# A hybrid encoder layer on one Trainium2 core: the last down-projection product goes row by row in a fixed order, and the work behind it is rearranged

## The chip, the cores and the metric

The kernel runs on 1 core of one Trainium2 chip. The metric is the device time of one execution in microseconds (us), lower is better. Before the change it is 1217.25 us, the median of 3 runs (1216.84 to 1219.11). The names of the engines are those of the profile: PE multiplies matrices, DVE (VectorE) and ACT (ScalarE) work on whole tiles of 128 partitions, POOL (GpSimd) does small things here, SP only issues DMAs. [...]

## The reference

One layer of an encoder on a sequence of 1024 rows of 1024 numbers, in f32. What matters here is its end, the feed-forward part and the final normalisation:

```python
def rmsnorm(x, w):
    xf = x.astype(jnp.float32)
    y = xf * lax.rsqrt(jnp.mean(xf * xf, axis=-1, keepdims=True) + EPS)
    return (y * w.astype(jnp.float32)).astype(x.dtype)

def conv_ffn(h, w_up, conv_w, w_down):
    u = causal_dwconv(h @ w_up, conv_w)
    g, val = jnp.split(u, 2, axis=-1)
    return (jax.nn.silu(g) * val) @ w_down
...
        h = rmsnorm(x, norm_ffn_w[l]) * (1 + sc_f) + sh_f
        x = x + g_f * conv_ffn(h, w_up[l], ffn_conv_w[l], w_down[l])
    return rmsnorm(x, final_norm_w)
```

So at the end each row of x gets g_f times a row of the product with w_down added (the gate and the residual), then the mean of its squares is taken over all 1024 columns, and the row is scaled by one over the root of that mean and by the weights of the last norm.

## The kernel before

**Precision.** Products are in f32 made of three matmuls with rounded operands: each operand is split into a high part (rounded, a copy on ACT, line 85) and a low part (the rest, a subtraction on DVE, line 86). `mm3` multiplies high by high (line 76), high by low (77) and low by high (78), and adds all three in one PSUM bank.

**The product with w_down.** It runs as one level of a Strassen-Winograd scheme: seven products of half size instead of eight, called P1, Q5, Q6, Q7, Q4, P3 and P2 in their order. Each has 11 steps of 128 in the inner dimension (`KH` = 11), over four row tiles of 128 rows (`R4`) and 512 columns. A step is 12 matmuls of 128x512: four row tiles by three. Steps go in pairs: a pair m = 0 to 4 holds two steps, pair 5 (`NM` - 1) has one (`kn(m)`). For each pair both operands, a of w_down and b of the hidden rows, are loaded, added where the scheme wants it (line 1371), and split into a buffer of a ring of five (`ring`, `wsplit`, `split_pair`). So with two buffers for a pair, a pair's second buffer is free when PE is done with the pair two before it. The banks "d" and "e" of four each take turns: a product fills one set while the other is emptied.

**What is made of the products.** The output has eight row tiles, 0 to 7, in two halves of 512 columns. `q5` becomes the right half of tiles 4 to 7, `u3` the right half of tiles 0 to 3, `u2` the left half of tiles 4 to 7 and `p1` the left half of tiles 0 to 3. `p1` without its last addend, `q5` and `u3` are finished early and gated there (`gate`: times g_f, plus the residual x, which is loaded from `x1d`). `u2` waits for P3 (banks `Z`), and `p1` for P2 (banks `W`), the last product. Row tiles 4 to 7 are therefore finished beside P2, and tiles 0 to 3 only after it.

**The end of a row tile** is `final`: ACT squares both halves, with the sum as by-product (line 1431; the squares themselves go into one of three output buffers, `fins[st % 3]`, as junk), DVE adds the two sums and the epsilon (line 977), POOL raises that to the power -1/2 (line 978), DVE scales each half by it and by the norm's weights `fnr` (line 1434), and SP issues a DMA for each half (line 1436).

**Order.** The order on each engine is not that of the code: a scheduler arranges the instructions by a simulated timeline and by what each waits for. Helpers like `issue_after` and the wrapper `InOrder` pin an order: while `V.on`, `A.on`, `T.on` are set (DVE, ACT, PE), each instruction of that engine follows the one written before it; line numbers of such instructions are shown as L58. Before the change the end of the down-projection is left to the scheduler. Each engine works through its queue in order, so an instruction that waits holds up what stands behind it.

Of the kernel before, what the change touches and what calls it, by code (L numbers as in the profile page):

```python
# [12 lines left out]
AF = mybir.ActivationFunctionType  # L13
# [3 lines left out]
P = 128  # L17
# [47 lines left out]
def tile_block(ctx: ExitStack, tc: tile.TileContext, x, crep, pk, w_ada, w_first, w_ft, w_z,  # L65
# [1336 lines left out]

    def product(p, ps, ready=(), tail=False, between=None):
        last = []
        for m in RM:
            ab = ready[m] if m < len(ready) else split_pair(p, m)
            if between:
                between(m)
            for k in range(2 * m, 2 * m + kn(m)):
                if tail and m >= NM - 2:  # L1410
                    last.append((ab, k))
                else:
                    step(ps, ab, k, R4)
        return last

# [10 lines left out]

    def final(st, lo, hi):
        t = fins[st % 3]
        m = [stat(), stat()]
        for dh, src in enumerate((lo, hi)):  # L1430
            A.activation(t[:, halves[dh]], src, AF.Square, scale=1.0 / 32.0, accum_out=m[dh])
        r = rstd2(m)
        for dh, src in enumerate((lo, hi)):
            V.scalar_tensor_tensor(t[:, halves[dh]], src, r, fnr[:, halves[dh]], op0=ALU.mult,
                                   op1=ALU.mult)
            nc.sync.dma_start(out[st * P:(st + 1) * P, halves[dh]], t[:, halves[dh]])

# [54 lines left out]
    Z = banks("e")  # L1492
    product("P3", Z)
    W = banks("d")
    last = product("P2", W, tail=True)
    for st in R4:
        V.tensor_tensor(u2[st], u2[st], Z[st], ALU.add)
    for st in R4:
        gate(u2[st], 4 + st, 0)
        final(4 + st, u2[st], q5[st])  # L1500
    for st in R4:
        for ab, k in last:
            step(W, ab, k, (st,))
        e = xt_()
        V.tensor_tensor(e, W[st], gf[:, halves[0]], ALU.mult)
        V.tensor_tensor(p1[st], p1[st], e, ALU.add)
        final(st, p1[st], u3[st])
    es_s.close()
# [53 lines left out]
```

## Time and profile before

| what | value |
|---|---|
| median of 3 runs | 1217.25 us |
| the profiled execution, its own time | 1217.67 us |
| its span, from the first to the last instruction | 1215.9 us |
| mean granted TensorE clock | 0.991 |
| product P2 on PE: first matmul starts, last one starts | 1171.85, 1201.54 us |
| last scaling on DVE starts | 1212.05 us |

The profiled execution is one of its own, beside the three runs; 1217.67 - 1215.9 = 1.77 us lie around its span. All times in a trace count from the span's start. In a row of the timeline stand the start, the duration, the engine, the line, the operation, the tiles written and read, the shape and the count; in square brackets how long the engine stood idle before it and what ended that.

### The profile page before, as it was taken

To read this page: it belongs to the slowest core of one execution; us is meant where nothing else is said; L and a number is where in the kernel's file an instruction comes from. 1 tells how busy PE (TensorE), PEld (TensorE's weight loads), DVE (VectorE), ACT (ScalarE), POOL (GpSimd) and SP (SyncE) were. 2 spreads that over 40 slices of the span, in tenths; PEclk is the share of its full clock that TensorE was granted. 3 is DMA by queue.
4 is the path that set the end of the run, shared out by engine and by line. 5 is a ranking of instruction groups with operands and counts; after the bars stand their busy time and mean duration, and the time that the engine had idled before them with its cause. 6 is when DMAs were issued, how large, how long until landed. Compare 5 with 4: busy or idle time off the path is not lost.

```text
span 1215.9 us, 15656 instructions
## 1 busy us (share of the span) xinstructions
PE 1162.3 (96%) x5802; PEld 976.8 (80%) x5802; DVE 942.3 (77%) x1413; ACT 594.9 (49%) x1001; POOL 195.2 (16%) x174
## 2 busy tenths in 40 slices
PE   5999999999999989999899999999999999999995
PEld 4887888778889978888688888888888888888884
DVE  7756455598697788747899988988889779766976
ACT  4637465663333657676454543444434445433443
POOL 1109373782210134200000000000000000000002
PEclk9999999999999999999999999999999999999998
DMA  9632121323554301141223223322333278733533
GB/s 355 237 94 83 36 74 39 129 81 127 174 174 157 104 18 36 61 147 53 70 80 129 96 104 130 118 81 87 105 130 112 91 265 293 261 118 125 169 117 138
DMA packets 56683, 151.91 MB, mean 125 GB/s; under 512 B 5664, under 2 KB 5792, under 8 KB 55200
## 3 DMA queue, kind: packets, MB, share of 16 engines
q1 hardware_dynamic: 49552, 126.54, 31.3%
q10 hardware_dynamic: 7056, 24.38, 5.0%
q8 instruction: 45, 0.74, 0.3%
q14 instruction: 30, 0.25, 0.1%
HBM read 117.61 MB, written 29.10 MB: 121 GB/s over the span
## 4 chain that ended last, share of the span: by engine, by line
PE 67%; DVE 7%; ACT 2%; DMA 1%; issue 1%; POOL 0%; DVEq 0%; POOLq 0%; SPq 0%; ACTq 0%
PE dn L76 6%; PE dn L77 6%; PE dn L78 6%; PE wops L702 6%; PE uY L76 5%; PE uY L78 5%; PE uY L77 5%; PE uZ L78 3%; PE uZ L77 3%; PE uZ L76 3%; PE uX L78 3%; PE uX L77 3%; PE uX L76 3%; PE s L76 2%; PE s L77 2%; PE s L78 2%
## 5 line engine op out<-in xcount | busy, mean ns | idle before, releaser
L978 POOL TENSOR_TENSOR st<-st,mhalf 128x1 f32<-128x1 f32 x16 | 12.7, 799 | 691.7 <-DVE st L977 680.3
L76 PE MATMUL dn<-w 128*128 128x512 f32 x308 | 111.9, 389 | 0.0
L77 PE MATMUL dn<-w 128*128 128x512 f32 x308 | 111.9, 389 | 0.0
L78 PE MATMUL dn<-w 128*128 128x512 f32 x308 | 103.3, 389 | 0.0
L76 PE MATMUL uY<-tH,w 128*128 128x512 f32 x256 | 99.7, 390 | 1.8 <-ACT w L58 1.8
L410 POOL TENSOR_SCALAR p<-p,st 128x640 f32<-128x640 f32 (+4 forms) x64 | 98.5, 1554 | 13.6 <-DVE st L409 10.4
L78 PE MATMUL uY<-tH,w 128*128 128x512 f32 x256 | 99.6, 389 | 0.0
L77 PE MATMUL uY<-tL,w 128*128 128x512 f32 x256 | 99.6, 389 | 0.0
L85 ACT ACTIVATE w<-ya 128x1024 fp32r<-128x1024 f32 (+1 forms) x41 | 39.1, 955 | 86.1 <-PE uY L78 80.8
L702 PE MATMUL wops<-hH,yhl 128*128 128x512 f32 x224 | 74.9, 403 | 2.6 <-ACT yhl L85 1.4
L78 PEld LDWEIGHTS dn<-w 128*128 128x128 f32 x308 | 57.8, 188 | 12.1
L76 PEld LDWEIGHTS dn<-w 128*128 128x128 f32 x308 | 57.8, 188 | 12.0
L77 PEld LDWEIGHTS dn<-w 128*128 128x128 f32 x308 | 57.8, 188 | 11.9
L85 ACT ACTIVATE pt<-tp 128x512 fp32r<-128x512 f32 (+2 forms) x72 | 36.6, 523 | 48.6 <-PE tp L436 19.7
L404 DVE CUSTOM_DVE_ANT_0 p<-s,bias 128x640 f32<-128x640 f32 (+4 forms) x64 | 40.6, 650 | 25.4 <-PE tp L439 8.5
L86 DVE TENSOR_TENSOR pt<-tp,pt 128x512 fp32r<-128x512 f32 (+2 forms) x72 | 41.9, 595 | 22.3 <-ACT pt L85 13.4
L76 PEld LDWEIGHTS uY<-tH,w 128*128 128x128 f32 x256 | 48.0, 188 | 12.1 <-ACT w L58 2.2
L77 PEld LDWEIGHTS uY<-tL,w 128*128 128x128 f32 x256 | 48.1, 188 | 10.0
L78 PEld LDWEIGHTS uY<-tH,w 128*128 128x128 f32 x256 | 48.1, 188 | 9.9
L85 ACT ACTIVATE w<-xs 128x1024 fp32r<-128x1024 f32 (+1 forms) x41 | 38.9, 952 | 32.4 <-PE uY L78 32.4
L702 PEld LDWEIGHTS wops<-hH,yhl 128*128 128x128 f32 x224 | 42.4, 191 | 11.9 <-ACT yhl L85 1.7
L76 PE MATMUL s<-hH,wh 128*128 128x512 f32 x128 | 50.6, 395 | 0.9 <-DVE ct L515 0.9
(472 smaller groups left out, 3426.8 us busy)
## 6 DMA issues: line engine op xcount, KB each, us to landing
gz<-a ACTq DMA_DIRECT2D x10, 1024.0 KB, 5.3
wos<-in_w_ada_dram SPq DMA_DIRECT2D x18, 512.0 KB, 4.1
ya<-in_w_up_dram SPq DMA_DIRECT2D x11, 768.0 KB, 4.2
xs<-in_w_up_dram SPq DMA_DIRECT2D x11, 768.0 KB, 4.4
adat<-in_w_ada_dram SPq DMA_DIRECT2D x16, 512.0 KB, 6.4
raws<-in_w_ft_dram SPq DMA_DIRECT2D x16, 512.0 KB, 3.6
qk<-in_w_ada_dram SPq DMA_DIRECT2D x14, 512.0 KB, 4.4
gy<-a ACTq DMA_DIRECT2D x10, 512.0 KB, 2.6
```

The costliest lines, as they stand in the source:

```text
L76: T.matmul(ps, lh, rh, start=start, stop=False, skip_group_check=more)
L77: T.matmul(ps, lh, rl, start=False, stop=False, skip_group_check=more)
L78: T.matmul(ps, ll, rh, start=False, stop=stop, skip_group_check=more)
L85: i = A.activation(hi, src, AF.Copy) if ehi is A else ehi.tensor_copy(hi, src)
L86: return i, elo.tensor_tensor(lo, src, f32(hi), ALU.subtract)
L404: V.tensor_tensor_reduce(out=dst, in0=src, in1=bsl, scale=-1.0, scalar=3e38, op0=ALU.add, op1=ALU.min, accum_out=nm)
L410: G.tensor_scalar(pv_, pv_, rr, None, op0=ALU.mult)
L702: i = op(*a, **k)
L978: G.tensor_tensor(r, ms, mhalf[:, 0:1], ALU.pow)
```

## The change

The end of the kernel is rewritten from product P3 on. Nothing is computed otherwise; the order, the engine of some steps and a few buffers are other.

- **Fixed order.** For all of P2 and what stands beside and behind it, DVE, ACT and PE take the order of the code (`V.on = A.on = T.on = True`). Splits are made two pairs ahead.
- **P2 by row tile at its end.** Pairs 4 and 5 (three steps) are multiplied row tile by row tile: nine matmuls for tile 0, then nine for tile 1, and so on. The code before was written that way too, but the scheduler had interleaved the tiles.
- **One ring buffer for pair 5.** A pair of one step keeps both operands in one buffer, in all seven products.
- **Gates moved up.** The gate of `u2` is applied to what is there before P3 (times g_f, plus x, in `p3_rows`), and P3's result gets its own product with g_f (`add_gated`). This adds four multiplications of 128x512 on DVE. The right halves' squares are also taken early: those of tiles 4 to 7 in P3, those of tiles 0 to 3 in P2, where POOL also adds the epsilon.
- **Squares as junk into PSUM.** In P2 the squares go into the used banks `Z` and `W` instead of the output buffers.
- **The last row tiles.** `u3` is multiplied with the norm's weights beside P2. Behind P2 DVE multiplies and adds for a tile (`add_gated`), ACT squares it, POOL adds the two sums and takes the power, ACT scales the right half and issues its DMA, DVE scales the left half, and SP issues that DMA. The next tile's square stands ahead of the tile's scaling (`row_out(st - 1)`).

On DVE the end of the program stood as follows, from the first instruction that reads the last product (banks dn_9392 to dn_9395 are tiles 0 to 3, xs is a scratch row, cg is `p1`, dnH1 is `u3`):

```order
L1505 TENSOR_TENSOR xs_2856<-dn_9392,ya_781 128x512
L1505 TENSOR_TENSOR xs_2856<-dn_9393,ya_781 128x512
L1506 TENSOR_TENSOR cg_5464<-cg_5464,xs_2856 128x512 x2
L1505 TENSOR_TENSOR xs_2856<-dn_9394,ya_781 128x512
L1505 TENSOR_TENSOR xs_2856<-dn_9395,ya_781 128x512
L977 SCALAR_TENSOR_TENSOR st1_72<-st1_72 128x1
L1506 TENSOR_TENSOR cg_5464<-cg_5464,xs_2856 128x512
L977 SCALAR_TENSOR_TENSOR st1_72<-st1_72 128x1
L1506 TENSOR_TENSOR cg_5464<-cg_5464,xs_2856 128x512
L1434 SCALAR_TENSOR_TENSOR xs_2856<-cg_5464,st1_72,xs_2856 128x512
L1434 SCALAR_TENSOR_TENSOR xs_2856<-dnH1_8212,st1_72,xs_2856 128x512
```

With the change DVE's end is this, where the banks of tiles 0 to 3 are dn_9402 to dn_9405 (the first row is the low parts of pair 5, the second `u3` times the norm's weights):

```order
L58 TENSOR_TENSOR w_9552<-dna0_8320,w_9552 128x512 x2
L58 TENSOR_TENSOR dnH1_8212<-dnH1_8212,xs_2856 128x512 x4
L58 TENSOR_TENSOR xs_2856<-dn_9402,ya_781 128x512
L58 TENSOR_TENSOR cg_5464<-cg_5464,xs_2856 128x512
L58 TENSOR_TENSOR xs_2856<-dn_9403,ya_781 128x512
L58 TENSOR_TENSOR cg_5464<-cg_5464,xs_2856 128x512
L58 SCALAR_TENSOR_TENSOR xs_2856<-cg_5464,st1_72,xs_2856 128x512
L58 TENSOR_TENSOR xs_2856<-dn_9404,ya_781 128x512
L58 TENSOR_TENSOR cg_5464<-cg_5464,xs_2856 128x512
L58 SCALAR_TENSOR_TENSOR xs_2856<-cg_5464,st1_72,xs_2856 128x512
L58 TENSOR_TENSOR xs_2856<-dn_9405,ya_781 128x512
L58 TENSOR_TENSOR cg_5464<-cg_5464,xs_2856 128x512
```

Behind that stand two more scalings, of the left halves of tiles 2 and 3. All four multiplications came first before; now a tile's scaling stands between the additions of the next tile and the multiplication of the one after it, and the right halves' scalings and the sums (L977) are gone from DVE.

On ACT the last instructions stood like this before:

```order
L1431 ACTIVATE xs_2856,st1_72<-ya_781 128x512
L1431 ACTIVATE ya_781,st1_72<-dnH1_8212 128x512
L85 ACTIVATE w_9525<-dna0_8320 128x512
L1431 ACTIVATE xs_2856,st1_72<-dnH1_8212 128x512 x2
L1431 ACTIVATE xs_2856,st1_72<-cg_5464 128x512 x2
L1431 ACTIVATE ya_781,st1_72<-cg_5464 128x512
L1431 ACTIVATE xs_2856,st1_72<-cg_5464 128x512
L1431 ACTIVATE xs_2856,st1_72<-dnH1_8212 128x512
```

With the change ACT's last instructions are these; a row that writes dn is a square, one that writes xs or ya is a right half that is scaled:

```order
L58 ACTIVATE dn_9402,st1_72<-cg_5464 128x512
L58 ACTIVATE dn_9403,st1_72<-cg_5464 128x512
L58 ACTIVATE xs_2856<-dnH1_8212,st1_72 128x512
L1434 DMA out_0_dram<-xs_2856 128x512
L58 ACTIVATE dn_9404,st1_72<-cg_5464 128x512
L58 ACTIVATE xs_2856<-dnH1_8212,st1_72 128x512
L1434 DMA out_0_dram<-xs_2856 128x512
L58 ACTIVATE dn_9405,st1_72<-cg_5464 128x512
L58 ACTIVATE ya_781<-dnH1_8212,st1_72 128x512
L1434 DMA out_0_dram<-ya_781 128x512
L58 ACTIVATE xs_2856<-dnH1_8212,st1_72 128x512
L1434 DMA out_0_dram<-xs_2856 128x512
```

The squares of the right halves (dnH1) have left the end, four scalings and four DMA issues have come to ACT, and no square writes an output buffer there any more.

On PE the last matmuls of the program stood interleaved over the four banks before:

```order
L76 MATMUL dn_9392<-w_9522,w_9525 128x512
L77 MATMUL dn_9392<-w_9522,w_9525 128x512
L76 MATMUL dn_9393<-w_9522,w_9525 128x512
L77 MATMUL dn_9393<-w_9522,w_9525 128x512
L76 MATMUL dn_9394<-w_9522,w_9525 128x512
L77 MATMUL dn_9394<-w_9522,w_9525 128x512
L77 MATMUL dn_9395<-w_9516,w_9519 128x512
L78 MATMUL dn_9395<-w_9516,w_9519 128x512
L78 MATMUL dn_9392<-w_9522,w_9525 128x512
L78 MATMUL dn_9393<-w_9522,w_9525 128x512
L78 MATMUL dn_9394<-w_9522,w_9525 128x512
```

Now they go tile by tile, six matmuls of pair 4 and three of pair 5 for each:

```order
L58 MATMUL dn_9402<-w_9510,w_9513 128x512 x6
L58 MATMUL dn_9402<-w_9552 128x512 x3
L58 MATMUL dn_9403<-w_9510,w_9513 128x512 x6
L58 MATMUL dn_9403<-w_9552 128x512 x3
L58 MATMUL dn_9404<-w_9510,w_9513 128x512 x6
L58 MATMUL dn_9404<-w_9552 128x512 x3
L58 MATMUL dn_9405<-w_9510,w_9513 128x512 x6
L58 MATMUL dn_9405<-w_9552 128x512 x3
```

The number of matmuls is the same. The core of the diff:

```diff
     def split_pair(p, m):
-        ab = [wsplit(t, kn(m)) for t in operands(p, m)]
+        if kn(m) == 1:
+            w = ring()
+            ab = [w[:, :, j:j + 1, :] for j in range(2)]
+            for t, src in zip(ab, operands(p, m)):
+                last_split[:] = split(t[:, 0], t[:, 1], src, A, V)
+        else:
+            ab = [wsplit(t, kn(m)) for t in operands(p, m)]
...
+    def mean(src, junk):
+        m = stat()
+        A.activation(junk, src, AF.Square, scale=1.0 / 32.0, accum_out=m)
+        return m
+
+    def store(q, st, dh):
+        q.dma_start(out[st * P:(st + 1) * P, halves[dh]], fins[st % 3][:, halves[dh]])
+
+    def scale_row(st, src, r, dh):
+        V.scalar_tensor_tensor(fins[st % 3][:, halves[dh]], src, r, fnr[:, halves[dh]], op0=ALU.mult,
+                               op1=ALU.mult)
+        store(nc.sync, st, dh)
...
+    def p3_rows(m):
+        if m < 4:
+            gate(u2[m], 4 + m, 0)
+            mh[4 + m] = mean(q5[m], fins[m % 3][:, halves[1]])
+
+    product("P3", Z, between=p3_rows)
     W = banks("d")
-    last = product("P2", W, tail=True)
+    V.on = A.on = T.on = True
+    V.last = A.last = T.last = None
+
+    def add_gated(t, ps):
+        e = xt_()
+        V.tensor_tensor(e, ps, gf[:, halves[0]], ALU.mult)
+        V.tensor_tensor(t, t, e, ALU.add)
+
+    ml = {}
+    ab = [split_pair("P2", m) for m in range(2)]
+    for m in RM:
+        rs = {}
+        if m == 0:
+            for st in R4:
+                add_gated(u2[st], Z[st])
+                ml[4 + st] = mean(u2[st], Z[st])
+        elif m < 3:
+            rs = {st: rstd2([ml[4 + st], mh[4 + st]]) for st in (2 * m - 2, 2 * m - 1)}
+        if m + 2 < NM:
+            ab.append(split_pair("P2", m + 2))
+        for st in rs:
+            scale_row(4 + st, u2[st], rs[st], 0)
+            scale_row(4 + st, q5[st], rs[st], 1)
+            mh[st] = mean(u3[st], Z[st])
+            G.tensor_scalar(mh[st], mh[st], EPS, None, op0=ALU.add)
+        if m == 4:
+            for st in R4:
+                V.tensor_tensor(u3[st], u3[st], fnr[:, halves[1]], ALU.mult)
+        if m < NM - 2:
+            for k in range(2 * m, 2 * m + 2):
+                step(W, ab[m], k, R4)
+    rs = {}
+
+    def row_out(st):
+        A.activation(fins[st % 3][:, halves[1]], u3[st], AF.Copy, scale=rs[st])
+        store(nc.scalar, st, 1)
+        scale_row(st, p1[st], rs[st], 0)
+
     for st in R4:
-        V.tensor_tensor(u2[st], u2[st], Z[st], ALU.add)
-    for st in R4:
-        gate(u2[st], 4 + st, 0)
-        final(4 + st, u2[st], q5[st])
-    for st in R4:
-        for ab, k in last:
-            step(W, ab, k, (st,))
-        e = xt_()
-        V.tensor_tensor(e, W[st], gf[:, halves[0]], ALU.mult)
-        V.tensor_tensor(p1[st], p1[st], e, ALU.add)
-        final(st, p1[st], u3[st])
+        for k in range(2 * NM - 4, KH):
+            step(W, ab[k // 2], k, (st,))
+        add_gated(p1[st], W[st])
+        m, rs[st] = mean(p1[st], W[st]), stat()
+        G.tensor_tensor(m, m, mh[st], ALU.add)
+        G.tensor_tensor(rs[st], m, mhalf[:, 0:1], ALU.pow)
+        if st > 0:
+            row_out(st - 1)
+    row_out(3)
```

More of the change, by code (lines that the diff above doesn't have):

```diff
@@ L1401, in step, with product @@
             mm3(ps[st], b[:, 0, c], b[:, 1, c], a[:, 0, :], a[:, 1, :], k == 0, k == KH - 1)
-    def product(p, ps, ready=(), tail=False, between=None):
-        last = []
+    def product(p, ps, ready=(), between=None):
         for m in RM:
@@ L1409, in product @@
             for k in range(2 * m, 2 * m + kn(m)):
[L1410 to L1414, printed above, removed]
+                step(ps, ab, k, R4)
     def xt_():
@@ L1425, in gate @@
         V.tensor_tensor(t, t, x, ALU.add)
[L1427 to L1436, printed above, removed]
+    def mean(src, junk):
[8 more added lines that the diff above has]
+        store(nc.sync, st, dh)
     def rows(ts):
@@ L1492, in tile_block @@
     Z = banks("e")
[L1493 to L1507 removed]
+    mh = {}
```

## The prediction

> **What bounds the kernel now.** I read the page first, then the busy time of the last stages by windows, then the timeline of each engine behind the last product.
>
> ```profile
> span 1215.9 us, 15656 instructions
> PE 1162.3 (96%) x5802; PEld 976.8 (80%) x5802; DVE 942.3 (77%) x1413; ACT 594.9 (49%) x1001; POOL 195.2 (16%) x174
> 1010.00:1020.00 10.00, 10.00 (x46) 8.28 (x45) 10.00 (x10) 3.35 (x5) 0.00 (x0) 1.00 0.95 351
> 1190.00:1200.00 10.00, 10.00 (x46) 8.29 (x45) 5.01 (x8) 4.03 (x11) 2.47 (x2) 1.00 0.41 154
> 1200.00:1205.00 5.00, 1.93 (x9) 1.27 (x7) 4.17 (x8) 1.34 (x4) 0.34 (x1) 0.97 0.00 0
> 1205.00:1216.00 11.00, 0.00 (x0) 0.00 (x0) 6.48 (x13) 2.17 (x6) 2.36 (x4) 0.50 0.51 191
> ```
>
> In a window's row the second number is PE's busy time, the fourth DVE's, the fifth ACT's, the sixth POOL's; the last three are the granted clock, the DMA share and GB/s. PE is busy 96% of the span and wholly so until 1200, at full clock, so there is nothing to win ahead of the last matmul, only something to lose. Behind it PE has nothing left, and DVE works 6.48 of the last 11 us. That tail is what the change can shorten.
>
> ```profile
> 1171.85 0.39 PE L76 MATMUL dn<-w 128*128 128x512 f32 x1
> 1201.54 0.39 PE L78 MATMUL dn<-w 128*128 128x512 f32 x1
> 1200.83 1.29 DVE L1505 TENSOR_TENSOR xs<-dn,ya 128x512 f32<-128x512 f32 x2 [4.71 <-PE dn L78]
> 1202.04 1.28 DVE L1506 TENSOR_TENSOR cg<-cg,xs 128x512 f32<-128x512 f32 x2
> 1203.24 1.28 DVE L1505 TENSOR_TENSOR xs<-dn,ya 128x512 f32<-128x512 f32 x2
> ...
> 1205.78 0.74 DVE L1434 SCALAR_TENSOR_TENSOR xs<-cg,st,xs 128x512 f32<-128x512 f32 x1
> ...
> 1208.43 0.14 DVE L977 SCALAR_TENSOR_TENSOR st<-st 128x1 f32<-128x1 f32 x1
> 1209.24 0.75 DVE L1434 SCALAR_TENSOR_TENSOR ya<-cg,st,xs 128x512 f32<-128x512 f32 x1 [0.66 <-POOL st L978]
> ...
> 1211.38 0.75 DVE L1434 SCALAR_TENSOR_TENSOR xs<-cg,st,xs 128x512 f32<-128x512 f32 x1 [0.66 <-POOL st L978]
> 1212.05 0.75 DVE L1434 SCALAR_TENSOR_TENSOR xs<-dnH,st,xs 128x512 f32<-128x512 f32 x1
> 1208.66 0.63 ACT L1431 ACTIVATE xs<-cg 128x512 f32<-128x512 f32 x1 [2.72 <-DVE st L977]
> 1209.20 0.19 ACT L1431 ACTIVATION_READ_ACCUMULATOR xs<-cg 128x1 f32 x1
> ```
>
> The first two rows are the first and last of P2's 132 matmuls: (1201.54 - 1171.85) / 131 = 0.2266 us from one to the next. The last ends at 1201.54 + 0.39 = 1201.93. DVE sits idle for 4.71 us and begins only at 1200.83, because the four tiles come out of PE together. Then it has all four tiles to do at once: two instructions of 128x512 start 1.21 us ahead of the next two, so 0.60 each; a scaling takes 0.66 from start to start. It ends at 1212.05 + 0.75 = 1212.80, 10.87 behind PE, and 3.1 us later the span ends (DMA issue, landing, end of program). ACT's square of tile 3 waits 2.72 us. The row names L977, but that had long ended; tile 0's left scaling ends at 1205.78 + 0.74, its store lands 2.0 us on (next fence), at 1208.5, and the square starts at 1208.66: its junk goes into the buffer which that store reads. Together the tail is 1215.9 - 1201.93 = 13.97 us.
>
> ```profile
> out_dram<-xs SPq DMA_DIRECT2D x12, 256.0 KB, 2.0
> 1183.66 2.65 POOL L978 TENSOR_TENSOR st<-st,mhalf 128x1 f32<-128x1 f32 x2 [612.89 <-DVE st L977]
> 1189.86 2.07 POOL L978 TENSOR_TENSOR st<-st,mhalf 128x1 f32<-128x1 f32 x1 [3.54 <-DVE st L977]
> 1208.66 0.55 POOL L978 TENSOR_TENSOR st<-st,mhalf 128x1 f32<-128x1 f32 x1 [2.39 <-DVE st L977]
> 1189.70 1.22 DVE L86 TENSOR_TENSOR w<-dnL,w 128x1024 fp32r<-128x1024 f32 x1
> 1190.83 0.68 DVE L86 TENSOR_TENSOR w<-dna,w 128x512 fp32r<-128x512 f32 x1
> L116 POOL TENSOR_SCALAR st<-st x16: 213/255/634, 7.9 to 513.0; 128x1 f32<-128x1 f32 x16
> ```
>
> POOL's power takes 0.55 us alone. The one at 1189.86 took 2.07: it ends at 1191.93, 0.42 behind the second of two DVE subtractions of tiles in SBUF (1190.83 + 0.68 = 1191.51). So such DVE work holds POOL up, and I let a POOL operation that falls beside it end 0.42 after it.
>
> **The change part by part.** *PE.* The last product has the same 132 matmuls, so PE's last end stays at 1201.93 if nothing comes late. With the tiles one after the other, tile 3 ends there and tiles 2, 1 and 0 end 9, 18 and 27 matmuls earlier: 1199.9, 1197.9, 1195.8. Runs of 76, 77, 78 into one bank are in the old trace already at this pace, so I cost the new order of matmuls at nothing.
>
> *DVE up to tile 0.* Pair 4's second ring buffer is free when PE is done with pair 2; ACT's split of it starts then, also in the old trace:
>
> ```profile
> 1188.41 1.06 ACT L85 ACTIVATE w<-dnL 128x1024 fp32r<-128x1024 f32 x1 [2.82 <-issue]
> 1020.06 0.68 DVE L1148 TENSOR_TENSOR ya<-ya,xs 128x512 f32<-128x512 f32 x1
> 1020.66 0.68 DVE L1150 TENSOR_TENSOR xs<-xs,ya 128x512 f32<-128x512 f32 x1
> ```
>
> 72 matmuls from 1171.85 end at 1188.3, and the row has 1188.41. ACT ends at 1189.47, and DVE's low part runs 1189.5 to 1190.7. The power for tile 6 stands beside this DVE work, so it comes at 1190.7 + 0.42 = 1191.1. Then DVE does four scalings (tiles 6 and 7, 4 x 0.66: 1193.8), pair 5's two low parts (2 x 0.60: 1195.0) and four multiplications of `u3` (4 x 0.60: 1197.4). PE needs the second low part at 1195.4, one matmul ahead of tile 0's end: it comes 0.3 us early. The second and third row show that an instruction which reads what the one before it wrote starts 0.60 behind it, so a multiplication and its addition cost 1.2.
>
> *The tail.* DVE reaches tile 0 at 1197.4, 1.6 late: DVE, not PE, is the bound from here. Tile 0: multiply 1197.4, add 1198.0; tile 1: 1198.6 and 1199.2, done at 1199.9. ACT squares tile 0 from 1198.7 (0.54 + 0.19 by its two rows). POOL's addition for tile 0 is held up by tile 1's: 1199.9 + 0.42 = 1200.3, and the power 0.55 + 0.03 behind it: 1200.9. DVE scales tile 0 (to 1201.55), multiplies and adds tile 2 (to 1202.75), scales tile 1 (its power came at about 1202.0; to 1203.4), multiplies tile 3, and adds it from 1204.0 to 1204.7. Now the last chain: square 0.73 (1205.45), POOL's addition and power with their releases 1.15 (1206.6), ACT's and DVE's scalings side by side 0.75 (1207.4). With the same 3.1 us behind it the span ends at 1210.5, which is **5.4 us less**.
>
> What goes is thus 5.4 of the 10.87: four right-half scalings (2.6) and four sums (0.3) leave DVE's tail, two tiles are multiplied and added under PE, and the wait of 2.72 on the store is gone, since squares write PSUM. What comes is POOL's second operation on the chain (0.55) and DVE being 1.6 late.
>
> *Not shown by the trace.* POOL's addition of two single columns: between 0.25 (the median of L116, the scalar addition) and 0.55 (the power); I take 0.55, the same kind of instruction. It counts twice, so 0.6 less is possible. The power for tile 6 may slip in between two subtractions: 0.4 less. A square that writes PSUM: between 0.52 (ACT copies out of PSUM, four in 2.07 us, third row of the next fence) and the 0.73 of a square with its read into SBUF; I take 0.73. The Trainium skill (ScalarE: Activation LUTs, section "Step-by-step: what each stage is for") says PSUM is the faster destination for ACT; no run here shows it, and by that the sum would be shorter by no more than the bound just given.
>
> *Hidden.* The four added multiplications (2.4 us of DVE) and the gates of `u2` stand in P3 and P2, where DVE has room: 5.01 of 10 in the window from 1190, and PE covers it. In P2 the adds of `Z` stand ahead of pair 2's split: low part of pair 1 done and DVE free at 1172.7 (buffer free at 1169.3 as P3's pair 4 ends, two ACT copies, two subtractions), eight instructions to 1177.5, the last square 0.63, two ACT copies 1.9, low parts to 1181.7. PE needs that one at 1171.85 + 50 x 0.2266 = 1183.2. So 1.5 us are left there; without that cover each us costs one.
>
> *DMA issues on ACT.*
>
> ```profile
> 1020.74 1.04 ACT L85 ACTIVATE w<-dnt1h 128x1024 fp32r<-128x1024 f32 x1
> 1020.77 0.33 ACTq L1149 DMA_DIRECT2D gy<-ya  x1
> 1021.76 2.07 ACT L1464 ACTIVATE cg<-dn 128x512 f32<-128x512 f32 x4
> DMA to landing us min/median/max: 2.0/2.6/5.3
> ```
>
> An issue on ACT runs beside ACT's work, and the next instruction starts without a gap. Tile 1's store waits for its scaling and stands ahead of tile 3's square, but both are done by 1204.7. SP has four issues fewer, one of them the last but one, so by the 0.33 of an issue at most 0.3 is gained. The last row is of the loads and stores of x1d.
>
> **A rule of the skill.** The slow powers above fit the Trainium skill (SBUF — State Buffer, section "Who interferes with whom"): a DVE instruction with two inputs in SBUF and a GpSimd instruction that reads SBUF exclude each other, the first to start keeps the shared ports to its end. The trace agrees for POOL behind DVE (2.07 against 0.55). The rule also says that POOL can hold up DVE, which no row here shows; it is the first rival below.
>
> **The rivals.**
> 1. *POOL and DVE block each other in every tile.* If a tile's POOL pair never ends before the next tile's addition plus 0.42 + 0.58, each scaling comes 1.0 behind that addition. For tile 1 that is 1203.85 for 1202.75, so 1.1 later, and the last addition on POOL waits 0.25 more: gain 4.1. For it: the 2.07. Against: for tile 1 POOL has the gap from 1200.9 to 1202.15, in which DVE scales and reads PSUM. Time 1213.2.
> 2. *PE gets gaps.* The scheduler has reordered DVE in P1 too, and there it is busy 10.00 of 10.00 (the window from 1010). One DVE instruction of 1.2 us too late, three times, gives PE 3.6 us of gaps; two loads of x that land in 5.3 instead of 2.6, ahead of P2's splits, take 0.9 beyond the 1.5 of cover. Against: no wait of PE in the old trace, and one ring buffer less per product gives the splits more time. Gain 1.8: 1215.5.
> 3. *The change doesn't do what it says*: the output buffer again. Tile 3 uses tile 0's; its stores are issued at about 1201.6 and land by 1203.6, or 1206.9 at 5.3, which would cost 0.3. Time 1212.2.
> 4. *Slower: squares into PSUM are dear.* Nothing in this trace shows ACT writing PSUM. In P2 pair 2's split stands behind four of them on ACT: at x us each they end at 1174.0 + 4x, and the low part is there 3.4 later; PE stalls from x = 1.45. Each further us costs 4 there and 1 in the tail. The gain of 5.4 is gone at x = 2.4, and at x = 3 PE stalls 6.2 and the tail adds 2.3: 3.1 slower, 1220.4. Against: reading PSUM costs ACT no more than SBUF does (0.52).
>
> **How the numbers follow.** The sum is made against the profiled execution: 1217.67 - 5.4 = 1212.3. That execution is 0.42 above the median of the three runs, 1217.25, which is what the result will be set against, so 1211.9. The rivals' times are set down by the same median. The forecast has a chance of 0.72, rival 1 0.10, rival 2 0.10, rival 3 0.04, rival 4 0.04. The bounds of the unknown costs reach 1.0 to 1.3 below (1210.6); the three runs alone lie 0.4 below and 1.9 above their median. Upwards the range takes in rivals 1 and 3 and some of 2: 1210.6 to 1214.6. A measurement can tell about 0.2% (2.4 us) from no change; forecast and rivals 1 and 3 are beyond it: faster 0.86, within 0.2% most of rival 2: 0.09, slower 0.05.
>
> **What would show it.** Right: PE without gaps to its last matmul about 1202 into the span; DVE's first reading of P2 about 4 us ahead of that; the last DVE scaling 5.5 behind it (10.87 before); no ACT square waiting for an output DMA. Wrong: PE gaps at P2's pair 2 or 5 (late low parts), squares over 1 us, POOL operations of 2 us in the last tiles, or a last scaling that waits for something other than POOL.

## The result, and the profile after

| what | before | after |
|---|---|---|
| median of 6 runs each | 1217.45 us (1216.84 to 1221.3) | 1213.02 us (1211.37 to 1214.02) |
| ratio, 95% interval | 1 | 0.9958 [0.9945, 0.9971] |
| the profiled execution, its time and its span | 1217.67, 1215.9 us | 1214.02, 1212.3 us |
| PE's last matmul ends | 1201.93 | 1203.63 |
| tail: from there to the span's end | 13.97 | 8.67 |

The change makes the kernel faster: by 4.4 us by the medians, by 5.1 (3.5 to 6.7) by the ratio. The profiled execution after, at 1214.02, is the slowest of its six runs. The prediction was 1211.9 us in a range of 1210.6 to 1214.6, with a gain of 5.4 and a tail of 8.6. The tail is there almost to the digit; as the experiments show, two errors in it cancel.

The profiled execution after has these rows on the page and in the windows (columns as before the change: PE, PEld, DVE, ACT, POOL, clock, DMA share, GB/s):

```profile
span 1212.3 us, 15660 instructions
PE 1163.7 (96%) x5802; PEld 977.8 (81%) x5802; DVE 945.7 (78%) x1413; ACT 597.0 (49%) x1005; POOL 197.0 (16%) x182
1190.00:1200.00 10.00, 10.00 (x46) 8.29 (x45) 9.72 (x15) 3.33 (x7) 3.62 (x4) 1.00 0.41 153
1200.00:1205.00 5.00, 3.63 (x16) 2.66 (x15) 4.20 (x7) 3.00 (x8) 2.33 (x5) 1.00 0.27 103
1205.00:1213.00 8.00, 0.00 (x0) 0.00 (x0) 2.48 (x4) 2.54 (x5) 1.42 (x4) 0.60 0.53 198
```

The busy totals hardly moved (DVE 942.3 to 945.7): the work is the same, it stands elsewhere. In the window from 1190 DVE went from 5.01 to 9.72 of 10 us, under PE; in the last window it does 2.48 where it did 6.48. The timeline of PE, DVE, ACT and POOL at the end:

```profile
1191.68 11.95 PE L58 MATMUL dn<-w 128*128 128x512 f32 x52
...
1192.31 0.75 DVE L58 SCALAR_TENSOR_TENSOR xs<-cv,st,xs 128x512 f32<-128x512 f32 x1
...
1198.57 0.68 DVE L58 TENSOR_TENSOR xs<-dn,ya 128x512 f32<-128x512 f32 x1
1199.29 0.69 DVE L58 TENSOR_TENSOR cg<-cg,xs 128x512 f32<-128x512 f32 x1
...
1200.61 0.69 DVE L58 TENSOR_TENSOR cg<-cg,xs 128x512 f32<-128x512 f32 x1
1202.03 0.75 DVE L58 SCALAR_TENSOR_TENSOR xs<-cg,st,xs 128x512 f32<-128x512 f32 x1 [0.73 <-POOL st L1549]
...
1205.41 0.69 DVE L58 TENSOR_TENSOR cg<-cg,xs 128x512 f32<-128x512 f32 x1
...
1207.78 0.75 DVE L58 SCALAR_TENSOR_TENSOR xs<-cg,st,xs 128x512 f32<-128x512 f32 x1 [1.02 <-POOL st L1549]
...
1206.13 0.60 ACT L58 ACTIVATE dn<-cg 128x512 f32<-128x512 f32 x1 [0.65 <-DVE cg L58]
...
1207.50 0.34 ACTq L1434 DMA_DIRECT2D out_dram<-ya  x1
1207.94 0.72 ACT L58 ACTIVATE xs<-dnH,st 128x512 f32<-128x512 f32 x1 [0.47 <-POOL st L1549]
...
1200.88 0.47 POOL L1548 TENSOR_TENSOR st<-st 128x1 f32<-128x1 f32 x1 [7.10 <-ACT dn L58]
...
1202.14 0.69 POOL L1548 TENSOR_TENSOR st<-st 128x1 f32<-128x1 f32 x1
...
1206.93 0.19 POOL L1548 TENSOR_TENSOR st<-st 128x1 f32<-128x1 f32 x1 [1.17 <-ACT dn L58]
1207.20 0.55 POOL L1549 TENSOR_TENSOR st<-st,mhalf 128x1 f32<-128x1 f32 x1
```

PE runs without a gap to 1191.68 + 11.95 = 1203.63. DVE takes up tile 0 at 1198.57, 5.06 ahead of that (1.10 before: 1200.83 against 1201.93). The last chain is then short: the addition of tile 3 (1205.41), its square (1206.13), POOL's addition and power (1206.93, 1207.20), and the two scalings side by side, DVE's to 1208.53 and ACT's to 1208.66.

**Why the tail gained 5.3 and the span only 3.6.** PE's end came 1.70 later. That is not the change. The first matmul of line 76 into `uX`, in code that is the same in all these kernels, shows it. In the timeline of before:

```profile
611.53 0.39 PE L76 MATMUL uX<-b11h,w 128*128 128x512 f32 x1
```

In that of after:

```profile
613.18 0.39 PE L76 MATMUL uX<-b11h,w 128*128 128x512 f32 x1
```

After is 1.65 later already there, hundreds of us ahead of the changed code. In the experiments below the same matmul starts anywhere from 608.38 (first bytes early) to 615.41 (add from PSUM). The windows show how this arises. In before, from 430 us to that matmul:

```profile
430.00:611.00 181.00, 172.29 (x862) 143.59 (x861) 132.64 (x185) 113.97 (x243) 34.21 (x41) 0.98 0.19 65
```

In the execution that was there at 608.38:

```profile
430.00:608.40 178.40, 169.65 (x863) 141.59 (x862) 132.45 (x186) 113.72 (x243) 33.73 (x41) 1.00 0.19 65
```

The granted clock is 0.98 in the one and 1.00 in the other, and the same matmuls keep PE busy 172.29 and 169.65 us. The clock isn't lowered evenly. It is 1.00 nearly everywhere and drops to 0.50 for some 3.4 us at a time: in before the windows of 2 us from 398 to 404 have 0.79, 0.50 and 0.86. Ahead of the `uX` matmul before has three such drops (near 400, 445 and 585 us), after has four, and the execution that was there at 608.38 has one. The fourth of after stands where before has none. First before, then after:

```profile
236.50:241.50 5.00, 3.95 (x29) 3.19 (x29) 3.35 (x10) 3.67 (x10) 5.00 (x4) 1.00 0.92 372
236.50:241.50 5.00, 4.66 (x28) 4.39 (x25) 2.64 (x8) 2.97 (x9) 5.00 (x3) 0.66 1.01 406
```

With three drops more than the execution at 608.38, after reaches the `uX` matmul 613.18 - 608.38 = 4.80 later, 1.6 for each drop; with one more than before, 1.65 later. What sets a drop off is not shown. So a single execution of any of these kernels lies some us up or down with the clock that was granted in the middle of the program. One execution per kernel can't judge a us by its time, but it can by its tail, which starts anew at PE's end. The experiments are read by the tail. Spans are given to 0.1, and three kernels with the same chain behind PE (the changed one, squares in buffers, store on SP) have tails of 8.62 to 8.67, so 0.3 is clear and 0.1 is not.

### The profile page after: what moved, and what is told of

The parts are those of the page before. It is cut to its first block, busy times and chain, and to the rows that moved or that the text cites. A ratio compares the mean times of both kernels' runs of the same rounds, so it can differ in the third digit from the quotient of the medians.

```text
span 1212.3 us, 15660 instructions
## 1 busy us (share of the span) xinstructions
PE 1163.7 (96%) x5802; PEld 977.8 (81%) x5802; DVE 945.7 (78%) x1413; ACT 597.0 (49%) x1005; POOL 197.0 (16%) x182
## 4 chain that ended last, share of the span: by engine, by line
PE 67%; DVE 7%; ACT 2%; DMA 1%; issue 1%; POOL 0%; SPq 0%; ACTq 0%; DVEq 0%; POOLq 0%
PE wops L702 6%; PE dn L76 5%; PE dn L78 5%; PE dn L77 5%; PE uY L76 5%; PE uY L77 5%; PE uY L78 5%; PE uZ L77 3%; PE uZ L76 3%; PE uZ L78 3%; PE uX L77 3%; PE uX L78 3%; PE uX L76 3%; PE s L76 2%; PE s L77 2%; PE s L78 2%
## 5 line engine op out<-in xcount | busy, mean ns | idle before, releaser
L978 POOL TENSOR_TENSOR st<-st,mhalf 128x1 f32<-128x1 f32 x12 | 9.8, 822 | 672.9 <-DVE st L58 625.0
L77 PE MATMUL dn<-w 128*128 128x512 f32 x264 | 97.8, 389 | 0.0
L76 PE MATMUL dn<-w 128*128 128x512 f32 x264 | 97.2, 389 | 0.0
L78 PE MATMUL dn<-w 128*128 128x512 f32 x264 | 92.1, 389 | 0.0
L78 PEld LDWEIGHTS dn<-w 128*128 128x128 f32 x264 | 49.6, 188 | 10.4
L77 PEld LDWEIGHTS dn<-w 128*128 128x128 f32 x264 | 49.6, 188 | 10.3
L76 PEld LDWEIGHTS dn<-w 128*128 128x128 f32 x264 | 49.5, 188 | 10.2
```

The costliest lines, as they stand in the source:

```text
L76: T.matmul(ps, lh, rh, start=start, stop=False, skip_group_check=more)
L77: T.matmul(ps, lh, rl, start=False, stop=False, skip_group_check=more)
L78: T.matmul(ps, ll, rh, start=False, stop=stop, skip_group_check=more)
L978: G.tensor_tensor(r, ms, mhalf[:, 0:1], ALU.pow)
```

## The experiments

Each is the changed kernel with one edit, if nothing else is said. PE's end is the start of the last group of matmuls in the timeline plus its duration.

| kernel | PE's end | span | tail | time (median) |
|---|---|---|---|---|
| the changed kernel | 1203.63 | 1212.3 | 8.67 | 1213.02, 6 runs |
| tiles together | 1193.63 + 12.18 = 1205.81 | 1217.5 | 11.69 | 1215.56, 10 runs |
| scheduler's order | 1201.93 + 0.39 = 1202.32 | 1212.2 | 9.88 | 1213.94, one |
| no square ahead | 1193.71 + 8.55 = 1202.26 | 1216.2 | 13.94 | 1216.91, 10 runs |
| squares in buffers | 1193.62 + 10.36 = 1203.98 | 1212.6 | 8.62 | 1214.35, one |
| right halves on DVE | 1193.70 + 7.42 = 1201.12 | 1210.4 | 9.28 | 1212.09, one |
| two ring buffers | 1184.82 + 17.44 = 1202.26 | 1211.5 | 9.24 | 1213.18, one |
| u3 in P3 | 1184.84 + 18.29 = 1203.13 | 1210.8 | 7.67 | 1211.32, 6 runs |
| add from PSUM | 1184.80 + 21.02 = 1205.82 | 1214.2 | 8.38 | 1215.9, one |
| last right half on DVE | 1189.66 + 12.40 = 1202.06 | 1210.8 | 8.74 | 1212.5, one |
| store on SP | 1189.77 + 11.27 = 1201.04 | 1209.7 | 8.66 | 1211.42, one |
| first bytes early (on u3 in P3) | 1189.78 + 9.00 = 1198.78 | 1206.3 | 7.52 | 1210.34, 6 runs |

### What the gain hangs on: the tiles' order on PE

```diff
+    for k in range(2 * NM - 4, KH):
+        step(W, ab[k // 2], k, R4)
     for st in R4:
-        for k in range(2 * NM - 4, KH):
-            step(W, ab[k // 2], k, (st,))
         add_gated(p1[st], W[st])
```

> The changed kernel with the last three steps of P2 multiplied step by step over all four tiles, not tile by tile; all else as changed. The tail (end of the last matmul to the end of the span) was 13.97 us before and 8.67 changed. Theory A, the order of the tiles on PE is what lets DVE start early: tile 0 ends 9 x 0.2266 = 2.0 us ahead of PE's end where it was 6.1, so DVE's first multiplication moves from 5.06 ahead of PE's end to 2.0 ahead, and everything behind it with it: tail +3.0, 11.7 us, time about 1216. Rival B, the gain is the work taken off DVE (right halves and sums, 2.9 us): the order of tiles matters little, since DVE was 1.1 us late for tile 0 anyway; tail +0 to +1.

Measured: the tail is 3.02 longer, and against before the ratio is 0.9994 [0.998, 1.0008]: no difference left that the time can tell, though the tail is still 2.3 shorter than before. DVE's first row of the tail:

```profile
1203.80 0.69 DVE L58 TENSOR_TENSOR xs<-dn,ya 128x512 f32<-128x512 f32 x1 [2.98 <-PE dn L58]
```

DVE was ready at 1200.8 and waited 2.98 for PE, to begin 2.0 ahead of PE's end instead of 5.06. Theory A holds with its number.

The second kernel leaves the order of DVE, ACT and PE to the scheduler.

```diff
-    V.on = A.on = T.on = True
-    V.last = A.last = T.last = None
```

> The fixed order of DVE, ACT and PE is taken away at the end; all else of the change stays, and the scheduler decides. It then interleaves the tiles on PE and puts DVE's first four multiplications in pairs ahead of most scalings. Theory A (the fixed order carries part of the gain): DVE begins tile 0 about 1.1 us ahead of PE's end and has seven instructions of 0.60 to 0.66 up to the last addition's end, 4.4 behind PE; with square 0.8, POOL 0.8, scaling 0.75 and 3.7 for the store the tail is about 10.5 us, 1.8 more than 8.67. Rival B (the moved work alone carries the gain): tail 8.7 to 9.2.

Measured: tail 9.88, 1.21 longer. The fixed order carries part of the gain, less than theory A's 1.8. Its start was wrong: DVE began 2.9 ahead of PE's end, not 1.1, when tiles 0 and 1 were both done.

```profile
1199.41 1.29 DVE L1507 TENSOR_TENSOR xs<-dn,ya 128x512 f32<-128x512 f32 x2 [5.62 <-PE dn L78]
```

### The next tile's square ahead of the scaling

```diff
-        if st > 0:
-            row_out(st - 1)
-    row_out(3)
+        row_out(st)
```

> The changed kernel with each tile's scaling straight behind its own square and power, so that the next tile's multiplication stands behind it on DVE and its square behind it on ACT. Theory A, having the next tile's work in the gap of POOL's power is worth most of the gain: per tile DVE waits for square 0.73, POOL's addition and power with their releases 0.9, so 1.6 us of idle for each of tiles 0 to 2 where it had 0.73 once: about 3 x 1.6 - 0.7 = +4.1, tail 12.8, nearly the old time (1217). Rival B, work taken off DVE: DVE's work is the same as in the changed kernel, so tail +0 to +1 (1213 to 1214).

Measured: tail 13.94, 5.27 longer, ratio to before 0.9998 [0.9984, 1.0011]. The whole gain is gone. The rows of DVE's first and last scaling of the tail:

```profile
1200.39 0.75 DVE L58 SCALAR_TENSOR_TENSOR xs<-cg,st,xs 128x512 f32<-128x512 f32 x1 [1.77 <-POOL st L1549]
...
1211.68 0.75 DVE L58 SCALAR_TENSOR_TENSOR xs<-cg,st,xs 128x512 f32<-128x512 f32 x1 [1.68 <-POOL st L1549]
```

Between them stand two more of 1.68. DVE goes the round of square, sum and power once for each tile, (1211.68 - 1200.39) / 3 = 3.76 us, where the changed kernel pays it in full only at the end. Theory A was right in kind and 1.2 short in size.

### Where the squares go, and the ring buffer

```diff
-        m, rs[st] = mean(p1[st], W[st]), stat()
+        m, rs[st] = mean(p1[st], fins[st % 3][:, halves[0]]), stat()
```

> The changed kernel with the squares of the last four tiles written into the output buffers, as before the change, not into PSUM. By the prediction's sentence that the wait of 2.72 us is gone since squares write PSUM, it comes back: ACT's square of tile 3 waits for tile 0's left store, tail +1 to +2.7. Theory A': the order of tiles removed it. Tile 0's left half is scaled 4.1 us ahead of tile 3's square now, its store lands 2.0 to 2.7 us behind its issue, so it is done 0.6 us ahead of the square: tail +0.0 to +0.1.

Measured: tail 8.62, the same. The prediction put the loss of the 2.72 us wait on the store down to the squares in PSUM (the memory of the product banks, which PE writes and DVE and ACT read in these traces); that is refuted. Tile 3's square again writes the buffer of tile 0, but tile 0's left half is now scaled by 1203.15 (1202.40 + 0.75), ahead of the additions of tiles 2 and 3, and a store lands 2.0 to 2.7 us on in this run, so by 1205.9. ACT's row waits for the addition alone:

```profile
1206.51 0.63 ACT L58 ACTIVATE xs<-cg 128x512 f32<-128x512 f32 x1 [0.66 <-DVE cg L58]
```

It takes 0.63 into SBUF, against the 0.60 into PSUM shown above. The Trainium skill (ScalarE: Activation LUTs, section "Step-by-step: what each stage is for") calls PSUM the faster destination; the trace agrees, by 0.03 us, which the tail doesn't show.

The next kernel gives pair 5 two ring buffers again (`ab = [wsplit(t, kn(m)) for t in operands(p, m)]` in all cases).

> Pair 5 takes two ring buffers again, as before the change. Theory A (the single buffer is needed by the row-by-row end): the second buffer is free only when PE is done with pair 3, which is 36 matmuls of 0.2266 us or 8.2 us ahead of PE's end; ACT's copy (0.5) and DVE's low part (0.6) follow, so DVE's four multiplications of u3 start 0.5 us later than in the changed kernel, and tile 0 with them: tail 9.2 instead of 8.67, PE without gaps of over 0.3. Rival B (there is room): tail within 0.15 of 8.67. Rival C (PE itself waits for the late low part): a gap of 0.5 or more ahead of pair 5's first matmul for tile 0.

Measured: tail 9.24, 0.57 longer, as theory A has it: DVE's second low part of pair 5 waits for ACT, which waited for PE. PE has a gap of 0.49 too, which theory A excluded and rival C looked for at another place. It is at P2's pair 2:

```profile
1194.75 0.69 DVE L58 TENSOR_TENSOR w<-dna,w 128x512 fp32r<-128x512 f32 x1 [0.53 <-ACT w L58]
...
1171.35 11.49 PE L58 MATMUL dn<-w 128*128 128x512 f32 x50
1183.33 6.87 PE L58 MATMUL dn<-w 128*128 128x512 f32 x29 [0.49 <-DVE w L58]
```

After 50 matmuls of P2 the low part of pair 2 is missing. That is the place where the prediction saw 1.5 us of cover: with two buffers DVE is busy with the splits of pairs 0 and 1 until 1173.78, 2.4 behind P2's start, and only then begins to add P3's banks; with the change's single buffer it begins 0.8 behind P2's start, and PE doesn't wait. The gap moves PE's end by itself, so it adds to the 0.57 of the tail.

### Right halves on ACT, and what the end of the stores is worth

In the first kernel the right halves are scaled on DVE as before the change, and the four multiplications of `u3` are gone.

```diff
-        if m == 4:
-            for st in R4:
-                V.tensor_tensor(u3[st], u3[st], fnr[:, halves[1]], ALU.mult)
...
-        A.activation(fins[st % 3][:, halves[1]], u3[st], AF.Copy, scale=rs[st])
-        store(nc.scalar, st, 1)
         scale_row(st, p1[st], rs[st], 0)
+        scale_row(st, u3[st], rs[st], 1)
```

> The changed kernel with the right halves of tiles 0 to 3 scaled on DVE and stored by SP as before the change, and without the four early multiplications by the norm's weights, which that makes needless. Theory A: DVE gets 2.4 us less ahead of the tail and 2.6 more in it. Its first multiplication comes 1.0 earlier (then PE's tile 0 is the bound), each of three tiles adds 0.66 and the last one 0.66 behind the left half: tail +0.4 to +0.8, 9.1 to 9.5 us. Rival B, the 2.6 us of right halves taken off DVE are half the gain: tail +2.6, 11.3 us.

Measured: tail 9.28, 0.61 longer: theory A. The 0.61 is a balance. Without the four multiplications DVE begins tile 0 at 1195.04, 6.08 ahead of PE's end, as it does in the kernel with `u3`'s work beside P3 (below), which keeps the right halves on ACT and has a tail of 7.67. Against that one the right halves on DVE cost 9.28 - 7.67 = 1.61. The last two rows:

```profile
1205.84 0.75 DVE L58 SCALAR_TENSOR_TENSOR xs<-cg,st,xs 128x512 f32<-128x512 f32 x1 [0.71 <-POOL st L1545]
1206.51 0.75 DVE L58 SCALAR_TENSOR_TENSOR xs<-dnH,st,xs 128x512 f32<-128x512 f32 x1
```

The last scaling ends at 1207.26, 6.14 behind PE, where the changed kernel has 4.90 on DVE: 1.24 later, for 0.61 of tail. From the last scaling to the end of the span are 3.14 us here, as before the change (3.1), and 3.64 in the changed kernel (from ACT's scaling; 3.77 from DVE's). From the *first* scaling of tile 3 it is 1210.4 - 1206.59 = 3.81 here, 1212.3 - 1208.53 = 3.77 after, and before 1215.9 - (1211.38 + 0.75) = 3.77. The DMA view says why. For the changed kernel, its share of busy time from 1207.5 to 1213 in 40 slices of 0.1375 us, and the stores issued there with their size and landing time:

```profile
DMA  1899989899930299999999980000000000000000
out_dram<-ya ACTq DMA_DIRECT2D x1, 256.0 KB, 2.0
out_dram<-xs SPq DMA_DIRECT2D x1, 256.0 KB, 2.1
out_dram<-xs ACTq DMA_DIRECT2D x1, 256.0 KB, 2.6
```

For the kernel with the right halves on DVE, from 1206 to 1210.5 in slices of 0.1125 us:

```profile
DMA  9999893000002799999999999300000000000000
```

The last block of 9s is the two stores of tile 3. It lasts 10 slices in the first and 12 in the second, 1.4 us in both and without a hole: 0.52 MB at some 370 GB/s. Whether the second half is scaled beside the first or 0.66 behind it, the bytes of the two take one stretch of 1.4 us that begins with the first. To test that, tile 3's right half alone went to DVE, behind the left half:

```diff
+        if st < 3:
             A.activation(fins[st % 3][:, halves[1]], u3[st], AF.Copy, scale=rs[st])
             store(nc.scalar, st, 1)
         scale_row(st, p1[st], rs[st], 0)
+        if st == 3:
+            V.tensor_scalar(fins[0][:, halves[1]], u3[3], rs[3], None, op0=ALU.mult)
+            store(nc.sync, 3, 1)
```

> The changed kernel, with the right half of tile 3 alone scaled on DVE behind the left half (a plain product with the power, since u3 holds the weights), instead of beside it on ACT. Theory A (the bytes bound the end): the left half's store starts when it did, the right half's bytes queue behind it as they do now, and the tail stays at 8.67, within 0.15, with only 3.1 to 3.2 from the last scaling's end to the span's end instead of 3.6 to 3.8. Rival B (the end follows the last scaling): 0.5 to 0.66 later, tail 9.2 to 9.3.

```profile
1206.24 0.75 DVE L58 SCALAR_TENSOR_TENSOR xs<-cg,st,xs 128x512 f32<-128x512 f32 x1 [1.03 <-POOL st L1553]
1206.91 0.48 DVE L58 TENSOR_SCALAR xs<-dnH,st 128x512 f32<-128x512 f32 x1
```

Measured: tail 8.74, the same within 0.07, though the last scaling ends 1207.39 - 1202.06 = 5.33 behind PE, for 5.03 in the changed kernel (ACT's, 1208.66). Theory A holds, rival B falls, though by less than was written: this form of the scaling takes 0.48, not 0.66, so the last scaling came only 0.30 later, and B asks for 8.97 instead of 9.2 to 9.3. From the last scaling to the span's end are 3.4 for the same reason, not 3.1 to 3.2; from the first, 1210.8 - 1206.99 = 3.81. The Trainium skill says the same of the two queues (DMA: Bandwidth & Descriptors, section "Issuing engines are not separate DMA queues"): stores issued by two engines share the DMA engines, only issue time is saved.

The next kernel moves the store of tile 2's right half from ACT, where it stands ahead of tile 3's scaling, to SP.

```diff
-        store(nc.scalar, st, 1)
+        if st != 2:
+            store(nc.scalar, st, 1)
         scale_row(st, p1[st], rs[st], 0)
+        if st == 2:
+            store(nc.sync, st, 1)
```

> The changed kernel, with the store of tile 2's right half issued by SP (behind that of the left half) instead of by ACT ahead of tile 3's scaling there. Theory A (ACT's issue holds ACT's next instruction): tile 3's scaling on ACT starts within 0.05 of POOL's power instead of 0.16 behind it. By the bytes the tail changes by less than 0.1, since DVE's store starts the flow. Rival B (the issue runs beside ACT's work, and the 0.16 has another reason): the 0.16 stays. Rival C (ACT's scaling sets the end): tail 8.5.

```profile
1204.62 0.55 POOL L1552 TENSOR_TENSOR st<-st,mhalf 128x1 f32<-128x1 f32 x1
1205.20 0.72 ACT L58 ACTIVATE xs<-dnH,st 128x512 f32<-128x512 f32 x1 [0.32 <-POOL st L1552]
```

Measured: ACT's scaling starts 0.03 behind the power (1205.17), where in the changed kernel it started 0.19 behind it (1207.20 + 0.55 = 1207.75 to 1207.94), with the issue from 1207.50 to 1207.84 ahead of it. So the issue did hold ACT. The tail is 8.66: it costs nothing here, since DVE's store opens the flow. Theory A holds, rivals B and C fall.

### POOL beside DVE

```diff
-        add_gated(p1[st], W[st])
+        V.tensor_tensor(W[st], W[st], gf[:, halves[0]], ALU.mult)
+        V.tensor_tensor(p1[st], p1[st], W[st], ALU.add)
```

> For tiles 0 to 3 the product with g_f is written back into its PSUM bank, so that the addition behind it has one input in PSUM and one in SBUF instead of two in SBUF. Theory A (DVE work with two inputs in SBUF holds POOL up): POOL's additions of tiles 0 and 1, 0.47 and 0.69 us long in the changed kernel, fall to the 0.19 of tiles 2 and 3, DVE's wait for POOL ahead of tile 0's scaling falls from 0.73 to about 0.45, and all that follows comes 0.3 earlier: tail 8.4 instead of 8.67. Rival B (they are long for another reason, or lie off the chain): they stay at 0.4 or more, and the tail stays within 0.15 of 8.67.

```profile
1203.07 0.19 POOL L1549 TENSOR_TENSOR st<-st 128x1 f32<-128x1 f32 x1 [7.11 <-ACT dn L58]
1204.33 0.41 POOL L1549 TENSOR_TENSOR st<-st 128x1 f32<-128x1 f32 x1 [0.42 <-ACT dn L58]
1203.95 0.75 DVE L58 SCALAR_TENSOR_TENSOR xs<-cg,st,xs 128x512 f32<-128x512 f32 x1 [0.45 <-POOL st L1550]
```

Measured: tail 8.38, 0.29 shorter, and DVE's wait for POOL 0.45 instead of 0.73, as theory A has it. Tile 0's addition on POOL takes 0.19. Tile 1's still takes 0.41: it ends at 1204.74, 0.04 behind the scaling of tile 0 (1203.95 + 0.75 = 1204.70), which reads SBUF. In the changed kernel the two ended 0.05 behind a DVE instruction in the same way: 1201.35 for the addition that ends at 1201.30, and 1202.83 for the scaling that ends at 1202.78. With nothing of the kind beside it, POOL's addition takes 0.19 in all these kernels. That is the rule of the Trainium skill that the prediction weighed (SBUF — State Buffer, "Who interferes with whom"), now shown by taking an input away; it ends 0.05 behind DVE, not the 0.42 that the prediction took from a power.

### Two versions that go further

The squares of `u3` and its four multiplications are taken beside P3:

```diff
+        if m == 4:
+            for st in R4:
+                mh[st] = mean(u3[st], X[st])
+                G.tensor_scalar(mh[st], mh[st], EPS, None, op0=ALU.add)
+                V.tensor_tensor(u3[st], u3[st], fnr[:, halves[1]], ALU.mult)
...
-            mh[st] = mean(u3[st], Z[st])
-            G.tensor_scalar(mh[st], mh[st], EPS, None, op0=ALU.add)
-        if m == 4:
-            for st in R4:
-                V.tensor_tensor(u3[st], u3[st], fnr[:, halves[1]], ALU.mult)
```

> The squares of u3 (with their epsilon) and its four multiplications by the norm's weights are taken beside P3 instead of P2, so nothing stands between pair 5's low parts and tile 0 on DVE. Theory A (DVE's lateness sets the tail): in the changed kernel tile 0 is done by PE 6.1 us ahead of PE's last end, but DVE begins it 5.06 ahead, 1.0 late. Without the four multiplications it begins with PE, about 6.0 ahead, and the last addition is bound by PE: it starts 0.8 behind PE's end instead of 1.78. The tail from PE's last end to the span's end is 8.67 - 1.0 = 7.7 us. Rival B (POOL's powers, not DVE's lateness, set the pace of the tiles, each scaling waiting for its power): the gain is lost in longer waits for POOL; tail 8.4 to 8.7. Rival C (P3 has no room for 12 more instructions): PE gets gaps in P3 and the kernel is slower than the changed one by more than it gains.

```profile
1197.05 0.69 DVE L58 TENSOR_TENSOR xs<-dn,ya 128x512 f32<-128x512 f32 x1 [1.30 <-PE dn L58]
1203.17 0.69 DVE L58 TENSOR_TENSOR xs<-dn,ya 128x512 f32<-128x512 f32 x1
1206.27 0.75 DVE L58 SCALAR_TENSOR_TENSOR xs<-cg,st,xs 128x512 f32<-128x512 f32 x1 [1.02 <-POOL st L1549]
```

Measured: tail 7.67, 1.0 shorter, PE without gaps; 1211.32 us, 0.9953 [0.9937, 0.997] of before. DVE now waits 1.30 for PE ahead of tile 0 and takes up tile 3 at 1203.17, 0.04 behind PE's end: theory A, rivals B and C fall. So in the changed kernel DVE's lateness cost 1.0.

On top of this kernel, DVE scales the left half of tile 3 in two pieces of 256 columns with a store each.

> The kernel with u3's work beside P3 (tail 7.67 us), and here DVE scales the left half of tile 3 in two pieces of 256 columns, each stored by itself. Theory A (behind the last power it is the bytes that take the time: the two stores of 256 KB flow without a gap at some 380 GB/s, 1.4 us, so the end follows the first scaling that is done, 3.8 us on): the first piece is stored about 0.3 earlier, the last bytes flow 0.3 earlier, though the last scaling itself ends later by some 0.1: tail 7.3 to 7.5. Rival B (the end follows the last scaling by a fixed time): tail 7.7 to 7.9.

Measured: tail 7.52, 0.15 shorter; 1210.34 us, 0.9949 [0.9932, 0.9966] of before. It is on theory A's side, since the tail fell though the last DVE scaling ends later, but by half of what was written, and 0.15 is little beside spans that are given to 0.1; I take it as agreeing, no more. By their medians both kernels beat the changed one, but they were timed on two chips, each against before there, and the intervals of the three ratios overlap; that they are better rests on the tails.

## Why the prediction was right, point by point

- **PE's end stays.** Right for the mechanism: no wait on PE. The 1.70 by which it moved is the clock in code that is not touched, and belongs to this pair of executions. Over six runs each the gain is 4.4 by the medians and 5.1 by the ratio, for 5.4 predicted and 5.3 in the tail; what is left between them can't be split off from runs of the changed kernel that lie 2.6 apart.
- **DVE takes up tile 0 late.** Predicted 4.5 ahead of PE's end, measured 5.06. Tile 6's scaling started at 1192.31 without a wait: the power that was to block it for 0.42 had slipped in, the alternative that the prediction names. The lateness itself is right, and costs 1.0 (u3 in P3).
- **Tiles at 1.2 each.** A multiplication that reads PSUM and the addition behind it are 0.72 apart (1198.57, 1199.29), not the 0.60 of the two SBUF instructions they were costed by: 0.12 too little for each of the four tiles.
- **POOL's addition at 0.55.** Mis-sized: 0.19 alone, below the bound of 0.25. For tile 0 it was blocked by tile 1's addition, as predicted, and ended 0.05 behind it. The last addition on DVE begins 1.78 behind PE's end (2.1 predicted); square, POOL and scaling took 1208.53 - 1206.10 = 2.43, not 2.7. Together the last scaling ends 4.90 behind PE on DVE, 0.6 earlier than the 5.5 predicted.
- **The same 3.1 us behind the last scaling.** This is the step that failed: 3.77. The two last stores' bytes follow each other, so the end goes by the first scaling of the last tile, 3.7 to 3.85 us on, in before, after and every experiment that stores whole halves. The 0.6 lost here cancel the 0.6 won above: 4.90 + 3.77 = 8.67 for 5.5 + 3.1 = 8.6. That the sum is right to 0.1 is luck; that DVE's chain is the bound and what shortens it is not. By the first scaling the gain is 10.20 - 4.90 = 5.30.
- **The wait of 2.72 on the store is gone, since squares write PSUM.** The wait is gone; the reason was wrong (squares in buffers). Tile 0 is now scaled and stored ahead of the additions of tiles 2 and 3; how much of that is PE's order and how much DVE's was not taken apart.
- **What goes: right-half scalings and sums, 2.9.** Over-stated as a share. Taking the right halves off DVE is worth 0.6 by the experiment (1.6 where the four multiplications that it needs don't delay tile 0), the order of the tiles 3.0, the square ahead of the scaling 5.3; they overlap, so they don't add up. Without either of the latter two the time shows no gain any more. The gates and the right halves' squares that were moved up were put back in no run, so what they are worth alone is not shown.
- **DMA issues on ACT cost nothing.** Not so for ACT: an issue that waits for the copy just ahead of it held the next scaling 0.16. It costs the tail nothing.
- **Cover of 1.5 at pair 2.** About 1.0 by the row below: the low part is ready at 1183.89, and PE wants it 50 matmuls after P2's start (1203.24 - 131 x 0.2266 = 1173.56), at 1184.9. With two buffers it is gone.

```profile
1181.53 2.36 DVE L58 TENSOR_TENSOR w<-dnH,w 128x1024 fp32r<-128x1024 f32 x2 [1.74 <-ACT w L58]
```

- **The rivals.** The first came true for tile 0 only (DVE idle 0.73 there, none for tiles 1 and 2) and is worth 0.3, not 1.3. PE gaps, the output buffer and dear squares (0.60 measured, 2.4 needed) did not come.

## What to carry to other kernels

When a tail hangs on one engine, first look in which order the producer ends its tiles, and put the next tile's work into the round trip of the last one; here the first was worth 3.0 of the tail's 5.3 and the second all of it, while taking the right halves off the busy engine was worth 0.6, or 1.6 with the work that this needs out of the way. Measure the end of a kernel from the moment at which its first last-tile store can be issued: what was scaled up to 0.66 us later cost nothing here, since its bytes went behind those of the first. And compare tails, not spans, where the clock in an untouched stage moves the whole execution by more than the change is worth.

## What was not expected of the hardware

- Two stores of 256 KB, issued by SP and ACT at once, move no faster than two from SP 0.66 us apart: 1.4 us for both. The later one lands after 2.6 us, not 2.1.
- POOL's addition of two columns takes 0.19 us alone and 0.41 to 0.69 when it meets a DVE instruction that reads two inputs from SBUF; it ends 0.04 to 0.05 behind that instruction.
- The granted clock is 1.00 nearly everywhere and drops to 0.50 for some 3.4 us at a time, three times in the profiled execution of before ahead of 611 us, four times in that of after, once in that of first bytes early. The mean granted clock of the profiled executions lay between 0.988 and 0.997, and PE reached the same matmul of an unchanged program part between 608.4 and 615.4 us.
